# Experts' weights laid out by consecutive rows, token rows and gate products stored to match, one low part in four of the up projections on GpSimd

## The chip, the cores and the metric

The kernel runs on one core of a Trainium2 chip. The metric is device time in microseconds (us) of one launch. Before the change the median of three runs is 2925.77 us (2919.05 to 2926.43). One more execution was taken with the hardware profiler; all rows below come from it. Engines are named as in the profile: PE (TensorE), ACT (ScalarE), DVE (VectorE), POOL (GpSimd), SP (SyncE, which here only issues DMAs).

## The reference, cut to what matters

The program is two transformer blocks on 1024 tokens of 1024 features, all in float32. The change touches the last stage alone, a mixture of 32 experts of which each token uses two:

```python
xf = _rmsnorm(h, norm_g).reshape(t, d)              # t = 1024 tokens, d = 1024
...                                                 # a router picks 2 of 32 experts for each token
def expert_block(args):
    xb, e = args                                    # 128 token rows of one expert
    hid = jax.nn.silu(xb @ w_gate[e]) * (xb @ w_up[e])   # 1024 -> 512, twice
    return hid @ w_down[e]                          # 512 -> 1024
...
y = jnp.zeros((t, d), out.dtype).at[token_of].add(out)   # scaled by the gate and added to the token
```

Each sum over features may run in any order of the features, if the rows of the weights and the columns of the tokens are taken in the same one.

## The kernel before, in words

**Precision.** Every float32 product is made of three fast matmuls (`mm3`, lines 197 to 199): each operand x is split into a high part, x rounded to the fast format, and a low part, x minus the high part. In the profile the high part of a weight is `wdh` (ACT, line 1762), the low part `wdl` (DVE, line 1763). One call of `expert_parts` makes both for a piece of 128 x 1024 numbers (two rows of 128 of the sum, 512 columns each). The tiles `wdh` and `wdl` have four buffers each, so the splitting runs at most four pieces ahead of PE.

**One expert** takes twelve pieces: four for the gate projection (`pg`), four for the up projection (`pu`), two times two for the down projection (`pd`). Each piece feeds six matmuls of 512 columns. Besides, PE transposes the gathered token rows (`xg`, line 1780) and the hidden rows (`hd`, line 1802); ACT and DVE split the results (`exh`, `exl`, `hdh`, `hdl`, lines 148 and 149, read from PSUM); ACT makes the silu (line 1798), DVE the product with the up projection (line 1799), and ACT scales the output rows `y` (line 1818). Two output halves of an expert are computed while the next expert's gate projection is already being split: the down projection of expert e-1 comes after the up projection of expert e.

**Order.** The framework orders each engine's instructions at build time; at run time each engine goes strictly in that order and waits on semaphores. In the first dozen experts DVE and PE also make, in small steps, a table for experts with more than 128 tokens (`overflow`, lines 1706 to 1736).

**Weights.** `expert_weights` loads each of the three matrices of an expert as two halves of 1 MB into a ring of 13 slots of 128 x 2048 numbers (SP's queue, line 1754; six of the loads go through POOL's queue). A slot is loaded again when all pieces of it have been split. In the view `(k p) n -> p k n` partition p gets rows p, p+128, p+256, ... of the matrix, so a half is four separate runs of 512 numbers (2 KB) in each partition for gate and up, two runs of 1024 numbers (4 KB) for down.

**Tokens.** `norm` (lines 1544 to 1551) writes the normalized rows `xf` in two halves with a GpSimd product (line 1550) and stores them to `d_xf`, eight tiles of 128 tokens. POOL gathers an expert's rows from there by an indirect DMA three experts ahead (`xg`, line 1768), and adds an expert's result to the output by another (`out<-y`, line 1819).

Of the kernel before, what the change touches and what calls it, by code (L numbers as in the profile page):

```python
# [8 lines left out]
F32 = mybir.dt.float32  # L9
# [4 lines left out]
AF = mybir.ActivationFunctionType  # L14
ALU = mybir.AluOpType
# [4 lines left out]
P = 128  # L20
# [31 lines left out]
class Kernel:  # L52
# [1483 lines left out]
    def ffn_rows(self, p, pst, rk, tab):  # L1536

        nc = self.nc

        rs, lgs = {}, {}  # L1540
        group = {t: g for g in ROUTED for t in g}

        def norm(t, z):
            r = rs[t] = self.tl(p, [P, 1], tag="rn", bufs=3)
            nc.vector.tensor_copy(r, self.rms_rstd(p, z, D, EPS2, self.tl(p, [P, D], BF, tag="scr", bufs=1)))
            x = self.tl(p, [P, D], tag="xf", bufs=1)
            for s in (slice(0, 512), slice(512, D)):
                u = self.tl(p, [P, 512], tag="nrow", bufs=2)
                nc.vector.tensor_scalar(u, z[:, s], r, None, op0=ALU.mult)
                nc.gpsimd.tensor_tensor(x[:, s], u, self.gffn[:, s], op=ALU.mult)  # L1550
            nc.gpsimd.dma_start(self.d_xf[t * P:(t + 1) * P], x)

        def logits(t, z):
            xt = self.tl(p, [P, 8, P], tag="xt", bufs=1)
            for i in range(2):
                ps = self.tl(pst, [P, 4, P], tag="tp", bufs=2)
                for j in range(4):
                    nc.tensor.transpose(ps[:, j], z[:, (4 * i + j) * P:(4 * i + j + 1) * P], self.ident)
                self.evac(i, xt[:, 4 * i:4 * i + 4], ps)
            pl = self.tl(pst, [P, 512], tag="lg", bufs=1)  # L1560
            for k in range(8):
                nc.tensor.matmul(pl[:, :36], xt[:, k], self.wr[:, k], start=k == 0, stop=k == 7)
            g = group[t]
            if t == g[0]:
                lgs[g] = self.tl(p, [P, len(g), 36], tag="lgs", bufs=2)
            nc.vector.scalar_tensor_tensor(lgs[g][:, t - g[0]], pl[:, :36], rs.pop(t), self.rb, op0=ALU.mult, op1=ALU.add)

        def place(t, z):
            g = group[t]
            if t == g[-1]:  # L1570
                self.route(p, lgs.pop(g), g)
                for x in g:
                    for y in range(x):
                        nc.tensor.matmul(rk[:, x], self.onesb, self.asum[:, y], start=y == 0, stop=False)
                    nc.tensor.matmul(rk[:, x], self.trib, self.asum[:, x], start=x == 0, stop=True)

                self.slots(p, g, rk, tab)
        return [norm, logits, place]

    def route(self, p, lg, tiles):  # L1580
# [157 lines left out]
    def expert_weights(self, src, after=None):  # L1738

        r = []  # L1740
        for w in src:
            w = w.rearrange("(k p) n -> p k n", p=P)
            k = w.shape[1] // 2
            r.append([])
            for i in range(2):
                x = self.tl(self.wp[0 if self.wslot < W0 else 1 + (self.wslot == W0 or self.wslot > W0 + 8)], [P, 2048], tag=f"w{self.wslot}").rearrange("p (k n) -> p k n", k=k)
                self.wslot = (self.wslot + 1) % W1
                queue = self.nc.sync
                self.early -= 1
                if after is not None and self.early < 0:  # L1750
                    self.nc.vector.tensor_copy(x[:, 0, 0:1], after)
                    queue = self.nc.gpsimd
                with self.tc.issue_after(self.behind) if self.early >= 0 and self.behind else nullcontext():
                    d = queue.dma_start(x, w[:, i * k:(i + 1) * k])
                self.behind = d.ins
                r[-1].append(x)
        return r

    def expert_parts(self, w):
        nc = self.nc  # L1760
        wh, wl = [self.tl(self.ep, [P, 2, 512], F32R, tag=n, bufs=4) for n in ("wdh", "wdl")]
        nc.scalar.copy(wh, w)  # L1762
        nc.vector.tensor_tensor(wl, w, wh.bitcast(F32), op=ALU.subtract)  # L1763
        return wh, wl

    def expert_gather(self, idx, xg):
# [17 lines left out]
    def expert_up(self, x, w, tag):  # L1784

        ps = self.tl(self.eps, [P, 512], tag=tag)
        for g in range(4):
            wh, wl = self.expert_parts(w[g // 2][:, 2 * (g % 2):2 * (g % 2) + 2])
            for j in range(2):
                k = 2 * g + j  # L1790
                self.mm3(ps, (x[0][:, k], x[1][:, k]), (wh[:, j], wl[:, j]), k == 0, k == 7)
        return ps

    def expert_hidden(self, pg, pu):
        nc = self.nc
        hd = self.tl(self.ep, [P, 512], tag="hd", bufs=2)
        hh, hl = [self.tl(self.ep, [P, 4, P], F32R, tag=n, bufs=2) for n in ("hdh", "hdl")]
        nc.scalar.activation(hd, pg, AF.Silu)
        nc.vector.tensor_tensor(hd, hd, pu, op=ALU.mult)
        ps = self.tl(self.ept, [P, 4, P], tag="tp")  # L1800
        for f in range(4):
            nc.tensor.transpose(ps[:, f], hd[:, f * P:(f + 1) * P], self.ident)
        self.split_gain(hh, hl, ps)
        return hh, hl
# [216 lines left out]
```

## Time and profile before

| | |
|---|---|
| median of 3 runs | 2925.77 us |
| profiled execution, its own time | 2920.82 us |
| its span in the trace | 2919.0 us |
| PE busy | 2759.6 us, 95% of the span |
| DVE busy | 1866.7 us, 64% |
| ACT busy | 1335.9 us, 46% |
| POOL busy | 468.6 us, 16% |
| DMA issued by SP | 377.69 MB, 225672 packets |
| stretch of the experts | about 2290 to 2919 us |

The shares are means over stages with different limits; the experts' stage, the last fifth of the span, has its own. There the outputs `out<-y` are issued by POOL once for each of the 32 experts, so the distance between two of them is the time that an expert takes.

### The profile page before, as it was taken

To read this page: it belongs to the slowest core of one execution; us is meant where nothing else is said; L and a number is where in the kernel's file an instruction comes from. 1 tells how busy PE (TensorE), PEld (TensorE's weight loads), DVE (VectorE), ACT (ScalarE), POOL (GpSimd) and SP (SyncE) were. 2 spreads that over 40 slices of the span, in tenths; PEclk is the share of its full clock that TensorE was granted. 3 is DMA by queue.
4 is the path that set the end of the run, shared out by engine and by line. 5 is a ranking of instruction groups with operands and counts; after the bars stand their busy time and mean duration, and the time that the engine had idled before them with its cause. 6 is when DMAs were issued, how large, how long until landed. Compare 5 with 4: busy or idle time off the path is not lost. (4 is left out here: it accounts for less than half of the span.)

```text
span 2919.0 us, 36892 instructions
## 1 busy us (share of the span) xinstructions
PE 2759.6 (95%) x13590; PEld 2168.0 (74%) x13590; DVE 1866.7 (64%) x3709; ACT 1335.9 (46%) x2295; POOL 468.6 (16%) x416
## 2 busy tenths in 40 slices
PE   7999999978999999999799999899999799999997
PEld 4875667756888888887686777688768688877776
DVE  6655554697534444437963767645555799988886
ACT  5644443512211221112333766624441488877776
POOL 0043201054101111103310100000003311111111
PEclk9999999989999999999999999999999899999999
DMA  8563333411211111111124212232235799999996
GB/s 283 178 200 106 112 106 120 137 54 51 65 37 50 58 58 44 48 44 61 66 96 130 87 55 80 69 131 102 65 119 195 263 353 348 346 345 349 350 347 216
DMA packets 245950, 432.55 MB, mean 148 GB/s; under 512 B 45924, under 2 KB 95492, under 8 KB 245384
## 3 DMA queue, kind: packets, MB, share of 16 engines
q1 hardware_dynamic: 225672, 377.69, 38.1%
q0 software_dynamic: 20096, 52.49, 5.6%
q8 instruction: 108, 1.77, 0.3%
q14 instruction: 74, 0.61, 0.1%
HBM read 380.79 MB, written 66.08 MB: 153 GB/s over the span
## 5 line engine op out<-in xcount | busy, mean ns | idle before, releaser
L1763 DVE TENSOR_TENSOR wdl<-w,wdh 128x1024 fp32r<-128x1024 f32 x384 | 458.1, 1222 | 63.1 <-ACT wdh L1762 57.3
L1762 ACT CAST wdh<-w 128x1024 fp32r<-128x1024 f32 x384 | 391.6, 1051 | 96.0 <-DMA w<-in_w_e_gate 38.9
L197 PE MATMUL mm<-whi,x 128*128 128x512 f32 (+1 forms) x1008 | 407.6, 405 | 20.0 <-DVE y L869 17.8
L198 PE MATMUL mm<-wlo,x 128*128 128x512 f32 (+1 forms) x1008 | 404.0, 401 | 1.5 <-DVE wlo L165 1.5
L199 PE MATMUL mm<-whi,x 128*128 128x512 f32 (+1 forms) x1008 | 401.2, 398 | 0.0
L164 ACT CAST whi<-raw 128x1024 fp32r<-128x1024 f32 (+1 forms) x111 | 113.9, 1044 | 401.3 <-PE m L199 263.7
L197 PE MATMUL mm<-x,whi 128*128 128x512 f32 (+1 forms) x592 | 233.7, 395 | 4.2 <-ACT relu L932 4.2
L165 DVE TENSOR_TENSOR wlo<-raw,whi 128x1024 fp32r<-128x1024 f32 (+1 forms) x111 | 158.4, 1433 | 119.7 <-ACT whi L164 118.3
L197 PEld LDWEIGHTS mm<-whi,x 128*128 128x128 f32 x1008 | 193.0, 191 | 55.1 <-DVE y L869 18.2
L199 PE MATMUL mm<-x,wlo 128*128 128x512 f32 (+1 forms) x592 | 232.1, 392 | 0.0
L198 PE MATMUL mm<-x,whi 128*128 128x512 f32 (+1 forms) x592 | 231.9, 392 | 0.0
L198 PEld LDWEIGHTS mm<-wlo,x 128*128 128x128 f32 x1008 | 192.7, 191 | 37.9 <-DVE wlo L165 4.1
L199 PEld LDWEIGHTS mm<-whi,x 128*128 128x128 f32 x1008 | 192.7, 191 | 34.1 <-issue 0.8
L981 DVE TENSOR_TENSOR acc<-acc,m 128x512 f32<-128x512 f32 x128 | 87.8, 686 | 195.4 <-PE m L199 195.2
L198 PE MATMUL m<-wlo,hidh 128*128 128x512 f32 x512 | 200.8, 392 | 0.5 <-DVE wlo L165 0.5
L199 PE MATMUL m<-whi,hidl 128*128 128x512 f32 x512 | 200.7, 392 | 0.0
L197 PE MATMUL m<-whi,hidh 128*128 128x512 f32 x512 | 200.3, 391 | 0.0
L970 POOL TENSOR_TENSOR raw<-raw,gt 128x1024 f32<-128x1024 f32 x32 | 85.8, 2694 | 516.8 <-DMA raw<-in_w_ff 516.8
L197 PEld LDWEIGHTS mm<-x,whi 128*128 128x128 f32 (+1 forms) x592 | 110.4, 186 | 30.1 <-ACT relu L932 5.2
L596 ACT ACTIVATE e<-sc,nm 128x256 f32<-128x256 f32 (+6 forms) x128 | 96.4, 755 | 79.0 <-PE tp L667 43.4
L199 PEld LDWEIGHTS mm<-x,wlo 128*128 128x128 f32 (+1 forms) x592 | 110.2, 186 | 25.2 <-issue 0.8
L198 PEld LDWEIGHTS mm<-x,whi 128*128 128x128 f32 (+1 forms) x592 | 110.3, 186 | 24.8 <-issue 1.1
(572 smaller groups left out, 5851.4 us busy)
## 6 DMA issues: line engine op xcount, KB each, us to landing
w<-in_w_e_gate SPq DMA_DIRECT2D x62, 1024.0 KB
w<-in_w_e_up SPq DMA_DIRECT2D x62, 1024.0 KB
w<-in_w_e_down SPq DMA_DIRECT2D x62, 1024.0 KB
raw<-in_w_ff SPq DMA_DIRECT2D x64, 512.0 KB
araw<-in_w_ada SPq DMA_DIRECT2D x48, 512.0 KB
raw<-in_w_in SPq DMA_DIRECT2D x36, 512.0 KB
raw<-in_w_ckv SPq DMA_DIRECT2D x16, 512.0 KB
x<-in_x SPq DMA_DIRECT2D x8, 512.0 KB
```

What stands on the lines that cost most here:

```text
L164: nc.scalar.copy(hi, raw)
L165: nc.vector.tensor_tensor(lo, raw, hi.bitcast(F32), op=ALU.subtract)
L197: mm(ps, lh, rh, start=start, stop=False)
L198: mm(ps, lh, rl, start=False, stop=False)
L199: mm(ps, ll, rh, start=False, stop=stop)
L596: nc.scalar.activation(e, ps, AF.Exp, bias=nm, accum_out=l)
L970: lambda raw: nc.gpsimd.tensor_tensor(raw, raw, gt, op=ALU.mult)) for f in range(4)]
L981: nc.vector.tensor_tensor(acc[t][:, ns], acc[t][:, ns], ps, op=ALU.add)
L1762: nc.scalar.copy(wh, w)
L1763: nc.vector.tensor_tensor(wl, w, wh.bitcast(F32), op=ALU.subtract)
```

## The change

Four edits, in the functions printed above.

1. The weights' view becomes `(p k) n -> p k n`: partition p gets k consecutive rows, so each half is a single run of 8 KB in each partition.
2. So that the token columns meet the same rows, `xf` is stored permuted: column p*8+k goes to place k*128+p. The GpSimd product writes with a stride of 128 numbers.
3. So that the hidden columns meet the rows of the down projection, silu and product are written to `hd` in the order f, p from columns p*4+f of PSUM, which are read with a stride of 4.
4. The third of the four pieces (g == 2) of the gate and of the up projection has its low part made by GpSimd in place of VectorE: two of an expert's twelve.

```diff
@@ norm, in ffn_rows
                 nc.vector.tensor_scalar(u, z[:, s], r, None, op0=ALU.mult)
-                nc.gpsimd.tensor_tensor(x[:, s], u, self.gffn[:, s], op=ALU.mult)
+                v = x.rearrange("r (k p) -> r p k", k=8)[:, s.start // 8:s.stop // 8]
+                nc.gpsimd.tensor_tensor(v, u.rearrange("r (p k) -> r p k", k=8),
+                                        self.gffn[:, s].rearrange("r (p k) -> r p k", k=8), op=ALU.mult)
             nc.gpsimd.dma_start(self.d_xf[t * P:(t + 1) * P], x)
@@ expert_weights
-            w = w.rearrange("(k p) n -> p k n", p=P)
+            w = w.rearrange("(p k) n -> p k n", p=P)
@@ expert_parts
-    def expert_parts(self, w):
+    def expert_parts(self, w, eng=None):
         wh, wl = [self.tl(self.ep, [P, 2, 512], F32R, tag=n, bufs=4) for n in ("wdh", "wdl")]
         nc.scalar.copy(wh, w)
-        nc.vector.tensor_tensor(wl, w, wh.bitcast(F32), op=ALU.subtract)
+        (eng or nc.vector).tensor_tensor(wl, w, wh.bitcast(F32), op=ALU.subtract)
@@ expert_up
-            wh, wl = self.expert_parts(w[g // 2][:, 2 * (g % 2):2 * (g % 2) + 2])
+            wh, wl = self.expert_parts(w[g // 2][:, 2 * (g % 2):2 * (g % 2) + 2], self.nc.gpsimd if g == 2 else None)
@@ expert_hidden
-        nc.scalar.activation(hd, pg, AF.Silu)
-        nc.vector.tensor_tensor(hd, hd, pu, op=ALU.mult)
+        blocks = lambda x: x.rearrange("r (p f) -> r f p", f=4)
+        hd4 = hd.rearrange("r (f p) -> r f p", f=4)
+        nc.scalar.activation(hd4, blocks(pg), AF.Silu)
+        nc.vector.tensor_tensor(hd4, hd4, blocks(pu), op=ALU.mult)
```

**POOL's queue in the middle of the experts.** `xg` is a gather, `out<-y` the adding of a result, `wdl` a low part. Before:

```order
L1768 DMA xg_19621<-d_xf,idx 128x1024
L1819 DMA out<-y_21332,idx 1024x1024
L1768 DMA xg_19622<-d_xf,idx 128x1024
L1819 DMA out<-y_21519,idx 1024x1024
L1768 DMA xg_19578<-d_xf,idx 128x1024
L1819 DMA out<-y_21706,idx 1024x1024
```

The same queue after the change:

```order
L1772 DMA xg_19622<-d_xf,idx 128x1024
L1767 TENSOR_TENSOR wdl_20867<-w_4325_20835,wdh_20866 128x1024
L1825 DMA out<-y_20770,idx 1024x1024
L1767 TENSOR_TENSOR wdl_20920<-w_4327_20839,wdh_20919 128x1024
L1772 DMA xg_19578<-d_xf,idx 128x1024
L1767 TENSOR_TENSOR wdl_21054<-w_4373_21022,wdh_21053 128x1024
L1825 DMA out<-y_20958,idx 1024x1024
L1767 TENSOR_TENSOR wdl_21107<-w_4375_21026,wdh_21106 128x1024
```

A gather and an output still alternate; a low part of a gate projection now stands before each output, one of an up projection before each gather.

**DVE's queue around the gate projection of one of the first dozen experts.** `exl` is the low part of token rows, `oh`, `val` and `acc` belong to the overflow table. The weights' slots are w_4612 (first half of the gate matrix), w_4613 (second half), w_4614 and w_4615 (up). Before:

```order
L149 TENSOR_TENSOR exl_21878<-tp_21886,exh_21877 128x512
L1763 TENSOR_TENSOR wdl_21969<-w_4612_21955,wdh_21968 128x1024
L1763 TENSOR_TENSOR wdl_21979<-w_4612_21955,wdh_21978 128x1024
L1763 TENSOR_TENSOR wdl_21989<-w_4613_21957,wdh_21988 128x1024
L1725 TENSOR_SCALAR oh_21948<-iota_18358,rf 128x128
L1727 TENSOR_SCALAR val_21949<-iota_18358,blk,iota_18364 128x16
L1727 TENSOR_SCALAR val_21949<-iota_18358,blk,ga 128x16
L1763 TENSOR_TENSOR wdl_21999<-w_4613_21957,wdh_21998 128x1024
L1730 TENSOR_TENSOR acc<-acc,tp_21941 128x32
L1763 TENSOR_TENSOR wdl_22022<-w_4614_21959,wdh_22021 128x1024
L1763 TENSOR_TENSOR wdl_22032<-w_4614_21959,wdh_22031 128x1024
L1763 TENSOR_TENSOR wdl_22042<-w_4615_21961,wdh_22041 128x1024
```

The same place on DVE after the change:

```order
L149 TENSOR_TENSOR exl_21878<-tp_21886,exh_21877 128x512
L1767 TENSOR_TENSOR wdl_21969<-w_4612_21955,wdh_21968 128x1024
L1767 TENSOR_TENSOR wdl_21979<-w_4612_21955,wdh_21978 128x1024
L1728 TENSOR_SCALAR oh_21948<-iota_18358,rf 128x128
L1730 TENSOR_SCALAR val_21949<-iota_18358,blk,iota_18364 128x16
L1730 TENSOR_SCALAR val_21949<-iota_18358,blk,ga 128x16
L1733 TENSOR_TENSOR acc<-acc,tp_21941 128x32
L1728 TENSOR_SCALAR oh_22129<-iota_18358,rf 128x128
L1730 TENSOR_SCALAR val_22130<-iota_18358,blk,iota_18364 128x16
L1730 TENSOR_SCALAR val_22130<-iota_18358,blk,ga 128x16
L1767 TENSOR_TENSOR wdl_21999<-w_4613_21957,wdh_21998 128x1024
L1767 TENSOR_TENSOR wdl_22022<-w_4614_21959,wdh_22021 128x1024
```

The third low part of the gate (from w_4613) is gone from DVE, and the table's small steps, which were spread among the low parts, now stand together in its place. ACT's and PE's queues keep their order, and SP issues the same loads in the same order.

## Rows read from the trace of the kernel before

**Rows 1.** The page: span, DMA share and GB/s in 40 slices.

```profile
span 2919.0 us, 36892 instructions
...
DMA  8563333411211111111124212232235799999996
GB/s 283 178 200 106 112 106 120 137 54 51 65 37 50 58 58 44 48 44 61 66 96 130 87 55 80 69 131 102 65 119 195 263 353 348 346 345 349 350 347 216
```

**Rows 2.** Windows of the experts' stage: busy us of each engine, clock, DMA.

```profile
core 0: us, PE busy (x) PEld busy (x) DVE busy (x) ACT busy (x) POOL busy (x), PEclk, DMA share, GB/s
...
2360.00:2560.00 200.00, 198.15 (x944) 162.33 (x943) 191.12 (x239) 167.03 (x196) 32.39 (x22) 1.00 0.99 349
2560.00:2880.00 320.00, 310.84 (x1411) 243.25 (x1409) 274.36 (x269) 249.16 (x300) 50.18 (x30) 1.00 0.99 348
```

**Rows 3.** Timeline of POOL: outputs of experts 0, 1, 12, 29, 30 (start, us).

```profile
2335.25 1.88 POOL L1819 DMA_INDIRECT out<-y,idx  x1 [4.40 <-ACT y L1818]
...
2352.98 1.82 POOL L1819 DMA_INDIRECT out<-y,idx  x1 [5.17 <-ACT y L1818]
...
2556.22 1.80 POOL L1819 DMA_INDIRECT out<-y,idx  x1 [5.17 <-ACT y L1818]
...
2882.43 2.03 POOL L1819 DMA_INDIRECT out<-y,idx  x1 [17.09 <-ACT y L1818]
...
2899.83 1.79 POOL L1819 DMA_INDIRECT out<-y,idx  x1 [15.38 <-ACT y L1818]
```

**Rows 4.** Waits from 2560 to 2880 us: total us, times, longest.

```profile
DVE wdl L1763 <- ACT wdh L1762: 42.9, 63, 2.3
ACT wdh L1762 <- DMA w<-in_w_e_gate: 33.8, 21, 2.6
...
ACT wdh L1762 <- DMA w<-in_w_e_up: 11.7, 17, 1.8
```

**Rows 5.** Waits from 2360 to 2560 us.

```profile
DVE wdl L1763 <- ACT wdh L1762: 6.3, 17, 1.5
ACT wdh L1762 <- DMA w<-in_w_e_gate: 5.0, 6, 2.0
```

**Rows 6.** Windows near the program's start, where DMA is full too.

```profile
18.00:20.00 2.00, 2.00 (x12) 1.67 (x11) 2.00 (x5) 1.01 (x3) 0.00 (x0) 1.00 1.02 420
...
28.00:30.00 2.00, 2.00 (x15) 0.60 (x14) 2.00 (x7) 1.26 (x4) 0.00 (x0) 1.00 1.05 383
```

**Rows 7.** SP's issues there: x has rows of 4 KB, raw and araw 2 KB.

```profile
12.08 3.80 SPq L414 DMA_DIRECT2D x<-in_x  x7
16.14 4.12 SPq L375 DMA_DIRECT2D araw<-in_w_ada  x4
21.18 3.18 SPq L160 DMA_DIRECT2D raw<-in_w_ckv  x3
```

**Rows 8.** DVE by line from 2560 to 2880 us: busy us, mean ns.

```profile
L1763 DVE TENSOR_TENSOR wdl<-w,wdh 128x1024 fp32r<-128x1024 f32 x199 | 235.3, 1221 | 44.9 <-ACT wdh L1762 42.9 <-PE pd L199 1.1
L149 DVE TENSOR_TENSOR exl<-tp,exh 128x512 fp32r<-128x512 f32 x34 | 21.8, 683 | 0.0
...
L1799 DVE TENSOR_TENSOR hd<-hd,pu 128x512 f32<-128x512 f32 x17 | 11.6, 680 | 0.0
```

**Rows 9.** Timeline of the feed-forward stage, POOL and DVE (start, us).

```profile
733.68 1.23 DVE L165 TENSOR_TENSOR wlo<-raw,whi 128x1024 fp32r<-128x1024 f32 x1 [0.26 <-ACT whi L164]
...
1136.84 2.39 POOL L970 TENSOR_TENSOR raw<-raw,gt 128x1024 f32<-128x1024 f32 x1 [74.09 <-DMA raw<-in_w_ff]
...
1147.01 2.76 POOL L970 TENSOR_TENSOR raw<-raw,gt 128x1024 f32<-128x1024 f32 x1 [1.43 <-DMA raw<-in_w_ff]
...
1147.77 3.08 DVE L165 TENSOR_TENSOR wlo<-raw,whi 128x1024 fp32r<-128x1024 f32 x1 [0.26 <-ACT whi L164]
```

**Rows 10.** Timeline of POOL: the last tile of xf, the first gather.

```profile
2280.39 2.77 POOL L1550 TENSOR_TENSOR xf<-nrow,gffn 128x512 f32<-128x512 f32 x2 [6.26 <-DVE nrow L1549]
2283.46 0.58 POOL L1551 DMA_DIRECT2D d_xf<-xf  x1 [0.30 <-POOL xf L1550]
...
2294.16 1.91 POOL L1768 DMA_INDIRECT xg<-d_xf,idx  x1 [9.16 <-DVE f L1710]
```

**Rows 11.** DMA issues by line: KB each, us to landing.

```profile
d_xf<-xf POOLq DMA_DIRECT2D x8, 512.0 KB, 4.2
```

**Rows 12.** ACT's silu by line, 2350 to 2880 us.

```profile
L1798 ACT ACTIVATE hd<-pg 128x512 f32<-128x512 f32 x28 | 16.8, 600 | 7.3 <-PE pg L199 7.3
```

## The prediction

> **What bounds the kernel now.** The page comes first. Its line of GB/s [rows 1] shows DMA far from full until the last fifth of the span and then flat near 348 GB/s, with nine tenths or more busy: the experts. All four edits touch that stage or what feeds it, so the rest of the program is left as it is.
>
> Next the pace of an expert, from the outputs that POOL issues once for each [rows 3]. From expert 0 to 12 it is (2556.22 - 2335.25) / 12 = 18.41 us, from 12 to 29 (2882.43 - 2556.22) / 17 = 19.19 us, then 17.40 us for the last distance. Over all 30 distances the mean is 18.82 us. The shortest shown is 17.73 us, from expert 0 to 1. I take it as what PE needs when nothing is late, since PE's busy time fills nearly all of the first window (198.15 of 200 us).
>
> Then the windows say which engine goes with which pace [rows 2]. Up to expert 12 PE has 99% and DVE 191.12 of 200 us: 96%, or 17.59 us per expert. So the first dozen are bound by PE and DVE together. Behind it DVE falls to 274.36 of 320 us, 16.45 us per expert, and PE shows gaps. The waits name the reason: ACT's split of a weight waits for the load of the gate matrix 33.8 us and of the up matrix 11.7 us [rows 4], against 5.0 us in the first window [rows 5]. There ACT is late because the weight is late, and DVE is late because ACT is (42.9 us against 6.3). The ring of 13 slots has run empty and the late experts go at DMA's pace: 348 GB/s times 19.19 us is 6.68 MB per expert. That fits: the weights are six transfers of 1 MB, and the rest is token rows.
>
> **Edit 1, the weights' layout.** It adds and removes no instruction; it turns four runs of 2 KB (two of 4 KB) per partition into one of 8 KB. No row shows 8 KB runs, so I bound the rate from rows where DMA is full too. In the middle of the 3.67 MB of x, rows of 4 KB, it moves 420 GB/s; a few us later, with the 2 KB runs of araw and raw, 383 GB/s [rows 6, 7]. The experts' own mix gives 348. If length does nothing, the rate stays 348 (19.19 us per expert). With 383 the 6.68 MB take 17.4 us, with 420 15.9 us. A loss cannot be excluded by rows, since consecutive runs also change which addresses are read together, but nothing points to one. I take 400 to 420: the runs become longer than those of x. At any rate over 6.68 / 17.73 = 377 GB/s the loads cease to set the pace, so what is taken above that does not matter.
>
> The page DMA: Bandwidth & Descriptors of the Trainium skill (section Where 436 GB/s comes from) speaks against this edit: between HBM and SBUF, it says, the HBM side at about 358 GB/s binds. By that rule the 348 is nearly the limit whatever the runs, and this edit gives nothing. The trace disagrees, with 420 GB/s for x [rows 6]; but those are other loads, so this case stays as a rival below.
>
> **Edit 4, low parts on GpSimd.** DVE loses two of twelve low parts: 2 x 1.22 = 2.44 us per expert [rows 8]. Alone this would make DVE quick: 17.59 becomes 15.15, 16.45 becomes 14.01. But the feed-forward stage shows what a GpSimd operation on two tiles of the same size does to a DVE operation on two. The low part there takes 1.23 us alone; begun 0.76 us after GpSimd's it takes 3.08 us, and it ends 1.08 us after GpSimd's end (1147.01 + 2.76 = 1149.77; 1147.77 + 3.08 = 1150.85) [rows 9]. It stood still until GpSimd was done. So each moved part takes 1.22 us from DVE and gives back up to GpSimd's whole duration, which is 2.39 us alone and 2.76 us in the disturbed case [rows 9].
>
> Without any cover DVE's sum is 16.45 - 2.44 + 2 x 2.39 = 18.79 us for late experts and 19.93 us for early ones (19.53 and 20.67 with 2.76). What can cover it: GpSimd's part runs beside DVE operations that are not held. All held ones in rows 9 have two inputs in SBUF. Four DVE operations of an expert read PSUM (two `exl`, `hdl`, the product `hd`), 0.68 us each [rows 8]. No row shows one of these beside GpSimd, held or not, so the cover is between 0 and 4 x 0.68 = 2.72 us. In the order, the low part of the gate's third piece follows close behind the two `exl` and DVE runs late there, so I expect half of those two to lie beside it: 0.68 us. In the early experts the table's small steps now stand together in that very place on DVE; they are the 17.59 - 16.45 = 1.14 us by which early DVE is fuller, and I let half of them be covered too. Late: 18.79 - 0.68 = 18.11, with handing over 18.2 us. Early: 19.93 - 0.68 - 0.57 = 18.68, taken as 18.6 us.
>
> [...]
>
> POOL's own queue bears the new work: some 2 x 2.4 us more in an expert of 18, where it is busy 32.39 of 200 us now [rows 2]. The gate's part is queued ahead of the output of the expert before, which has three buffers for `y`; the up projection's part stands behind that output, whose issue takes 1.8 to 2 us [rows 3]. That output waits for `y`, ready about when PE begins the next gate projection, so the part has the rest of a gate projection to be in time. A gather held back is three experts early.
>
> **Edits 2 and 3, the permuted stores.** Instruction counts stay; only strides change, and no row shows these strides. For `xf` the bounds are the 2.77 us that a tile's two products take now and twice that; the last tile is in memory at 2283.46 + 4.2 = 2287.7 us and the first gather starts at 2294.16 [rows 10, 11]. 6.5 us of cover hide 2.8 us. For silu (0.60 us [rows 12]) and product (0.68 us) the bounds are the same time and twice it; a gain is excluded, since no element is saved. Doubling would put 0.68 us on DVE per expert, 20 us over 30. I take no change, and 2 us for the whole of edits 2 and 3.
>
> **The sum.** Early: 12 x (18.6 - 18.41) = +2.3. Late: 17 x (18.2 - 19.19) = -16.8. Last distance: 18.2 - 17.4 = +0.8. With 2 us for the strides: -11.7 us, or 2909.1 against the profiled execution's 2920.82. That execution lies 4.95 us under the median, so against the median it is 2914 us. My first two terms are rounded against the change, so I state 2913.
>
> **The rivals.**
> 1. *The shared access decides* (slower). DVE and GpSimd never overlap. Early 12 x (19.93 - 18.41) = +18.2, late 17 x (18.79 - 19.19) = -6.8, last +1.4: +13 us, 2939; with 2.76 us per part +35 us, 2961. For it: rows 9, and DVE at 96% in the first window. Against: late DVE has 14% of idle time. It turns slower as soon as the mean over the 30 distances passes 18.82 us.
> 2. *The loads are not relieved.* 348 GB/s is a limit of something other than run length. Late experts stay at 19.19 us, and slower early ones merely leave the ring fuller: 0 to +5 us, 2928. For it: the flat 345 to 350 GB/s [rows 1]. Against: 420 in rows 6.
> 3. *Everything is covered.* The four PSUM operations lie beside GpSimd in full and PE alone binds. Late 17 x (17.73 - 19.19) = -24.8, early 12 x (18.0 - 18.41) = -4.9: -30 us, 2896. For it: late DVE would need only 18.79 - 2.72 = 16.1 us. Against: this needs each part to start just when such an operation comes.
>
> **How the numbers follow.** Chances: forecast 0.47 (its own range 2900 to 2925), rival 1 0.22, rival 2 0.16, rival 3 0.15. A measurement of this kernel tells about 0.3% from no change, 8.8 us: faster is under 2917, slower over 2934.5. Faster: 0.33 of the forecast's 0.47 and rival 3, 0.48. Slower: 0.17 of rival 1, 0.03 of rival 2, 0.02 of the forecast's upper tail, 0.22. The same: 0.30. The range of 2893 to 2943 takes in rival 3, rival 2 and rival 1 with the 2.39 us; the 2961 is left out.
>
> **What would show it.** Right: in the experts' windows GB/s over 377 or DMA's busy share under 0.95, no ACT wait for gate or up loads behind 2560 us, some DVE low parts of 2 to 3.5 us where GpSimd's run, late experts at about 18.2 us, early ones at 18.4 to 18.9. Wrong: GB/s flat at 348 with the waits for loads as before (rival 2); early experts over 19.5 us with DVE full (rival 1); DVE low parts all at 1.22 us, or GpSimd's part well over 2.8 us, which no term here holds.

## The result and the profile after

The median after is 2946.09 us (2945.58 to 2951.69, 4 runs) against 2922.41 (2917.96 to 2926.43, 4 runs): a ratio of 1.0087, 95% interval 1.0071 to 1.0103. That is slower by 0.9%, and outside the forecast range of 2893 to 2943. The profiled execution has a span of 2944.2 us, 25.2 more than before.

POOL's timeline, columns as in [rows 3], gives the outputs of experts 0, 4, 13, 20, 30 and 31 after the change.

```profile
2337.71 2.43 POOL L1825 DMA_INDIRECT out<-y,idx  x1 [0.17 <-ACT wdh L1766]
...
2414.32 2.41 POOL L1825 DMA_INDIRECT out<-y,idx  x1
...
2595.41 2.42 POOL L1825 DMA_INDIRECT out<-y,idx  x1 [0.15 <-ACT wdh L1766]
...
2722.74 2.39 POOL L1825 DMA_INDIRECT out<-y,idx  x1 [0.17 <-issue]
...
2924.01 1.77 POOL L1825 DMA_INDIRECT out<-y,idx  x1 [9.29 <-ACT y L1824]
2932.22 1.56 POOL L1825 DMA_INDIRECT out<-y,idx  x1 [6.44 <-issue]
```

Before, the outputs of experts 0 and 30 start at 2335.25 and 2899.83 [rows 3]; those of 4, 13, 20 and 31 are these:

```profile
2407.32 2.47 POOL L1819 DMA_INDIRECT out<-y,idx  x1 [5.17 <-ACT y L1818]
...
2575.16 1.88 POOL L1819 DMA_INDIRECT out<-y,idx  x1 [5.54 <-ACT y L1818]
...
2713.85 1.86 POOL L1819 DMA_INDIRECT out<-y,idx  x1 [8.17 <-ACT y L1818]
...
2906.98 1.55 POOL L1819 DMA_INDIRECT out<-y,idx  x1 [5.35 <-ACTq L1861]
```

The differences place the 25.2 us:

| stretch | before, us | after, us | difference |
|---|---|---|---|
| to the output of expert 0 | 2335.25 | 2337.71 | +2.5 |
| experts 0 to 4 | 72.07 | 76.61 | +4.5 |
| experts 4 to 13 | 167.84 | 181.09 | +13.3 |
| experts 13 to 20 | 138.69 | 127.33 | -11.4 |
| experts 20 to 30 | 185.98 | 201.27 | +15.3 |
| behind the output of expert 30 | 19.17 | 20.19 | +1.0 |

So the change gains among the later experts, where it was expected to gain, but for seven of them only (and the experiments show that it is hardly the new layout that makes these seven quick). The distances between outputs show three regimes: 20.34 to 20.40 us for each expert from 5 to 13, 18.18 to 18.20 from 13 to 20, and, after one of 15.98, 20.15 to 21.17 in the last nine up to expert 30. A window from each regime, columns as in [rows 2]:

```profile
2440.00:2560.00 120.00, 108.77 (x518) 88.75 (x518) 109.22 (x126) 91.08 (x105) 43.90 (x25) 1.00 0.85 313
2600.00:2720.00 120.00, 119.18 (x558) 97.09 (x557) 110.66 (x95) 101.85 (x120) 63.40 (x27) 1.00 0.97 366
2760.00:2880.00 120.00, 107.79 (x486) 84.06 (x485) 99.61 (x81) 86.96 (x104) 41.33 (x21) 1.00 0.85 327
```

In the middle PE is nearly full. In the other two it idles 11.23 and 12.21 of 120 us, and DMA is at 0.85, so the loads are not what is late; of ACT's waits for them [rows 4, 5] one is left between 2360 and 2880 us:

```profile
ACT wdh L1766 <- DMA w<-in_w_e_gate: 0.4, 1, 0.4
```

On the queue of the weights the packets fall from 225672 to 170120.

**Experts 5 to 13.** Waits from 2440 to 2560 us (total us, times, longest):

```profile
PEld tp L1731 <- DVE val L1730: 13.9, 6, 2.3
PE tp L1731 <- DVE val L1730: 11.2, 6, 1.9
```

PE's whole idle time of 11.23 us is one wait: six times, once in each expert, a matmul of the overflow table stands at the head of PE's queue and waits for DVE's `val`. The timeline of one such place shows why (start, us, engine; all rows but these four left out):

```profile
2450.19 2.50 POOL L1767 TENSOR_TENSOR wdl<-w,wdh 128x1024 fp32r<-128x1024 f32 x1 [4.01 <-ACT wdh L1766]
...
2450.38 2.39 DVE L1728 TENSOR_SCALAR oh<-iota,rf 128x128 f32<-128x128 f32 x1
...
2452.70 0.28 DVE L1730 TENSOR_SCALAR val<-iota,blk,iota 128x16 f32<-128x16 f32 x1
...
2453.23 0.41 PE L1731 MATMUL tp<-val,oh 128*128 128x32 f32 x2 [1.87 <-DVE val L1730]
```

`oh` is issued 0.19 us after GpSimd's low part and ends with it (2452.77 against 2452.69). It took 2.39 us here and 1336 ns on average over the window, since every second one is held; before it took 281 ns (first line: after, 2440 to 2560 us; second: before, 2360 to 2560):

```profile
L1728 DVE TENSOR_SCALAR oh<-iota,rf 128x128 f32<-128x128 f32 x12 | 16.0, 1336 | 0.0
...
L1725 DVE TENSOR_SCALAR oh<-iota,rf 128x128 f32<-128x128 f32 x15 | 4.2, 281 | 0.0
```

It is a small step of 128x128 numbers with one tile and one column of scalars as inputs. The table's matmul waits 1.87 us, and with it everything behind it in PE's queue: the rest of the gate projection.

Of the 4.5 us lost in experts 0 to 4, 3.2 lie in the one distance from expert 3 to 4 (21.32 us, before 18.11). There two steps that prepare the table are held in the same way, `hd` (before 0.69 us) and `blk` (before 0.17):

```profile
2390.75 2.65 DVE L1709 TENSOR_TENSOR hd<-ab,base 128x512 f32<-128x512 f32 x1
...
2396.30 2.38 DVE L1714 SCALAR_TENSOR_TENSOR blk<-f,blk 128x16 f32<-128x16 f32 x1
```

Behind them PE waits 2.5 us for DVE's low parts (2394 to 2416 us).

**Experts 20 to 30.** Waits from 2760 to 2880 us:

```profile
ACT hd L1804 <- PE pg L199: 17.3, 6, 3.1
...
PEld pu L198 <- POOL wdl L1767: 8.3, 6, 1.5
PEld pg L198 <- POOL wdl L1767: 8.0, 6, 1.9
...
PE pg L198 <- POOL wdl L1767: 6.5, 6, 1.5
PE pu L198 <- POOL wdl L1767: 5.7, 6, 1.0
```

6.5 and 5.7 are 12.2 us: again all that PE idles. Here it is GpSimd's low parts themselves that come late. The timeline of one gate projection:

```profile
2800.32 0.48 PE L197 MATMUL pg<-wdh,exh 128*128 128x512 f32 x1
2800.39 0.69 ACT L1824 ACTIVATE y<-pd,gate 128x512 f32<-128x512 f32 x1 [0.41 <-PE pd L199]
...
2801.05 0.58 ACT L148 CAST hdh<-tp 128x512 fp32r<-128x512 f32 x1
...
2801.54 3.89 ACT L1766 CAST wdh<-w 128x1024 fp32r<-128x1024 f32 x4
...
2802.68 2.70 POOL L1767 TENSOR_TENSOR wdl<-w,wdh 128x1024 fp32r<-128x1024 f32 x1
...
2805.43 0.50 PE L198 MATMUL pg<-wdl,exh 128*128 128x512 f32 x1 [1.00 <-POOL wdl L1767]
```

PE begins the projection at 2800.32, but ACT makes the high part of the third piece only behind `y` and `hdh`, at 2801.54; GpSimd's part runs from 2802.68 to 2805.38, and PE wants it at 2804.43. A part of DVE's 1.22 us [rows 8], begun at the same time, would end at 2803.9 (an estimate). Before the change ACT goes in this order here too (at one place `y` at 2767.97 us, `hdh` at 2768.55, the casts from 2769.01); what it costs without GpSimd's part is the subject of an experiment below.

**What stayed as expected.** By line, from 2560 to 2880 us, columns as in [rows 8]; silu is of 2350 to 2880 us, as in [rows 12], and GpSimd's part is the page's own row:

```profile
L1767 DVE TENSOR_TENSOR wdl<-w,wdh 128x1024 fp32r<-128x1024 f32 x165 | 238.3, 1486 | 39.7 <-ACT wdh L1766 39.7
L149 DVE TENSOR_TENSOR exl<-tp,exh 128x512 fp32r<-128x512 f32 x34 | 21.8, 680 | 0.0
...
L1805 DVE TENSOR_TENSOR hd<-hd,pu 128x512 f32<-128x512 f32 x16 | 10.8, 676 | 0.0
```

```profile
L1804 ACT ACTIVATE hd<-pg 128x512 f32<-128x512 f32 x27 | 16.2, 599 | 19.3 <-PE pg L199 19.3
```

```profile
L1767 POOL TENSOR_TENSOR wdl<-w,wdh 128x1024 fp32r<-128x1024 f32 x64 | 172.9, 2702 | 136.4 <-ACT wdh L1766 130.9
```

Silu and product cost the same with strides (599 and 676 ns against 600 and 680). DVE's low parts grew from 1221 to 1486 ns by the hold; GpSimd's takes 2.70 us. Over the whole stage DVE's low parts take 445.6 us where they took 458.1: of the 64 x 1.22 = 78 us that were moved, the holds on the other parts give 66 back.

### The profile page after: what moved, and what is told of

It reads as the page before. It is cut to its first block, busy times and chain, and to the rows that moved or that the text cites. A ratio compares the mean times of both kernels' runs of the same rounds, so it can differ in the third digit from the quotient of the medians.

```text
span 2944.2 us, 36983 instructions
## 1 busy us (share of the span) xinstructions
PE 2758.2 (94%) x13590; PEld 2172.3 (74%) x13590; DVE 1879.0 (64%) x3645; ACT 1340.3 (46%) x2295; POOL 641.1 (22%) x480
## 5 line engine op out<-in xcount | busy, mean ns | idle before, releaser
L1767 DVE TENSOR_TENSOR wdl<-w,wdh 128x1024 fp32r<-128x1024 f32 x320 | 445.6, 1432 | 67.1 <-ACT wdh L1766 67.1
L197 PE MATMUL mm<-whi,x 128*128 128x512 f32 (+1 forms) x1008 | 408.2, 405 | 19.3 <-DVE y L869 17.2
L1767 POOL TENSOR_TENSOR wdl<-w,wdh 128x1024 fp32r<-128x1024 f32 x64 | 172.9, 2702 | 136.4 <-ACT wdh L1766 130.9
L197 PEld LDWEIGHTS mm<-x,whi 128*128 128x128 f32 (+1 forms) x592 | 110.3, 186 | 28.4 <-ACT relu L932 4.0
## 6 DMA issues: line engine op xcount, KB each, us to landing
w<-in_w_e_gate SPq DMA_DIRECT2D x62, 1024.0 KB, 10.2
```

What stands on the lines that cost most here:

```text
L197: mm(ps, lh, rh, start=start, stop=False)
L1767: (eng or nc.vector).tensor_tensor(wl, w, wh.bitcast(F32), op=ALU.subtract)
```

## The experiments

The time at which POOL issues the first gather varies from 2291.2 to 2300.5 us between these executions, though they differ hardly at all up to there. So beside the medians I compare a stage, from the start of the first gather to the end of the span: 624.8 us before (2919.0 - 2294.16), 650.3 after (2944.2 - 2293.88). A stage is of the one profiled execution of each kernel. All ratios are to the kernel before on the same chip (its medians there are 2920.97 to 2923.33).

| kernel | median, us | ratio, 95% interval | stage, us |
|---|---|---|---|
| before | 2922.41 | | 624.8 |
| after | 2946.09 | 1.0071 to 1.0103 | 650.3 |
| edits 1 to 3 | 2906.59 | 0.9929 to 0.9962 | 607.6 |
| edit 4 alone | 2952.17 | 1.0092 to 1.0125 | 652.1 |
| after, table later | 2944.55 | 1.0069 to 1.0102 | 648.9 |
| after, POOL's order | 2948.62 | 1.0069 to 1.0107 | 649.7 |
| after, ACT's order | 2933.95 | 1.0022 to 1.0048 | 633.7 |
| after, `oh` on ACT | 2938.45 | 1.0040 to 1.0074 | 640.1 |
| after, both of these | 2922.99 | 0.9994 to 1.0014 | 624.1 |
| edits 1 to 3, ACT's order | 2902.33 | 0.9910 to 0.9943 | 605.1 |
| edits 1 to 3, both of these | 2902.65 | 0.9914 to 0.9947 | 606.2 |

The theory after the result: the layout by itself gains as forecast, and edit 4 loses more than that, by two separate waits on PE. The rivals: the layout itself costs something (its strides, its addresses); GpSimd's parts are late because of POOL's own queue; the table is late because of its place, not because of the hold.

**The two halves apart.** Edits 1 to 3 with all low parts on DVE:

```diff
-            wh, wl = self.expert_parts(w[g // 2][:, 2 * (g % 2):2 * (g % 2) + 2], self.nc.gpsimd if g == 2 else None)
+            wh, wl = self.expert_parts(w[g // 2][:, 2 * (g % 2):2 * (g % 2) + 2])
```

> Edits 1 to 3 alone, all low parts on VectorE. Theory A (the layout relieves the loads, the GpSimd parts cost all that was lost): no ACT wait for weights, experts 0 to 12 at about 18.4 us as before, later ones at 17.8 to 18.3 in place of 19.2, 15 to 24 us under the kernel before (2898 to 2908). Rival B (the strided silu, product and store cost): early experts over 18.8 us and silu or product longer than 0.60 and 0.68 us, time at 2922 or above. Rival C (run length does not matter to DMA): GB/s flat at 348, late experts at 19.2, same time as before.

And edit 4 put into the kernel before, with its old layout:

> Edit 4 alone on the old layout. Theory A: early experts with table steps at 20.4 us as in the changed kernel, the last ten at 20.4 too, the middle between 18.2 (while the ring, filled by the slow start, lasts) and 19.2: 20 to 35 us over before, 2942 to 2957. Rival B (the layout is what cost): within 0.3% of before.

The layout alone gives 0.9946, edit 4 alone 1.0108. The stage is 17.2 us shorter with the one and 27.3 longer with the other. In edit 4 alone the pace is 20.35 to 20.39 us for eight early experts and 18.17 to 18.20 for six in the middle, as after: these regimes belong to edit 4, whatever the layout. That holds for the quick middle too. With the old layout and 352 GB/s it has PE as full as after:

```profile
2600.00:2720.00 120.00, 119.05 (x556) 96.63 (x555) 109.14 (x94) 99.84 (x118) 63.95 (x26) 1.00 1.00 352
```

From expert 13 to 20 edit 4 alone takes 128.84 us, after 127.33, before 138.69. So 9.9 of the 11.4 us gained there need no new layout. While the early experts are slow the loads run ahead: from 2440 to 2560 us SP's queue waits 91.7 us for DVE's low parts to free a slot, before 19.3. Beside edit 4 the layout is worth 1.8 us of stage (652.1 to 650.3), without it 17.2.

The layout alone has 17.73 us where the table is done, with PE full and DMA at 373 GB/s:

```profile
2560.00:2660.00 100.00, 100.00 (x478) 83.14 (x478) 93.84 (x94) 86.24 (x103) 15.64 (x13) 1.00 0.98 373
```

Its waits from 2660 to 2880 us, where the last experts take 17.5 to 19.3 us, show that loads are late again, against the expectation, though less than before (13.2 of 220 us against 45.5 of 320 [rows 4]):

```profile
ACT wdh L1766 <- DMA w<-in_w_e_gate: 9.1, 6, 2.5
ACT wdh L1766 <- DMA w<-in_w_e_up: 4.1, 5, 1.2
```

DMA's share is 0.91 in this window, and SP's queue waits 126.7 us of it for DVE's low parts, that is, for a slot to come free. So the rate alone does not make them late.

**What run length does to the loads.** Two kernels whose experts compute so little that the loads alone set the pace, one in each layout:

```diff
-        nc.scalar.copy(wh, w)
-        (eng or nc.vector).tensor_tensor(wl, w, wh.bitcast(F32), op=ALU.subtract)
-        return wh, wl
+        self.flip = not getattr(self, 'flip', False)
+        nc.scalar.copy(wh, w) if self.flip else nc.vector.tensor_copy(wh, w)
+        return wh, wh
...
-                self.mm3(ps, (x[0][:, k], x[1][:, k]), (wh[:, j], wl[:, j]), k == 0, k == 7)
+                self.nc.tensor.matmul(ps, x[0][:, k], wh[:, j], start=k == 0, stop=k == 7)
```

> The old layout with the computing of the experts cut: only the high times high matmul of each piece, no low parts of weights, high parts by ACT and VectorE in turn, so that the loads bound the stage. Theory A (runs of 2 and 4 KB): GB/s in the stage near 350. Rival B (the 348 was the demand of a slower consumer, not DMA's limit): 380 or more.

> The same cut in the new layout. Theory A (8 KB runs are quicker): 380 to 420 GB/s, the stage 5 to 15% shorter than in the old layout. Rival B (run length does nothing): GB/s as in the old layout.

One run each. The windows of the old layout, then of the new one:

```profile
2360.00:2560.00 200.00, 113.85 (x402) 77.88 (x402) 80.06 (x168) 96.64 (x122) 28.39 (x22) 0.75 0.98 350
2560.00:2800.00 240.00, 139.34 (x440) 95.85 (x441) 80.97 (x125) 118.95 (x149) 33.66 (x24) 0.69 0.98 347
2320.00:2360.00 40.00, 21.37 (x96) 14.82 (x95) 16.60 (x28) 22.04 (x31) 11.13 (x9) 0.79 1.01 359
```

```profile
2360.00:2560.00 200.00, 125.26 (x414) 86.11 (x414) 82.70 (x172) 101.82 (x129) 28.36 (x23) 0.72 0.94 363
2560.00:2800.00 240.00, 140.01 (x453) 95.19 (x454) 82.85 (x127) 121.36 (x152) 35.10 (x25) 0.72 0.94 365
2320.00:2360.00 40.00, 26.96 (x112) 18.89 (x110) 19.02 (x32) 24.83 (x34) 12.66 (x11) 0.80 1.02 404
```

From 2320 to 2360 us, with DMA full in both, the new layout moves 404 GB/s and the old one 359. Behind that it moves 364 against 350 and 347, 4 to 5% more, but with DMA not quite full. Per full share, an estimate, that is 350 / 0.98 = 357 GB/s against 364 / 0.94 = 387: 8% more. The stage is 3.4% shorter (595.0 us against 615.8), under the expected 5 to 15%. So the layout does limit the loads; whether it does so by the length of the runs or by which addresses are read together, these two kernels do not separate. The 387 is under the 400 to 420 that the forecast took, and over the 377 that it needed.

**The table of the first dozen experts.** The changed kernel, with the table's steps moved behind expert 17:

```diff
-                if e > 1:
+                if e > 17:
                     next(more, None)
```

> The changed kernel with the table steps made during experts 18 to 30 in place of 2 to 14. Theory A (a table step held behind GpSimd's low part, with PE waiting for it, makes the early experts slow): experts 1 to 13 fall from 20.4 to about 18.2 us, experts 18 to 20 rise to 20.4, the last ten stay at 20.4 or rise by up to 2 us. Total between 15 us less and 10 us more than the changed kernel. Rival B (in the early experts the sum of VectorE and GpSimd is the bound, table or not): experts 1 to 13 at 19.9 us or more.

The first 17 distances fall to 18.18 to 18.20 us, and those that now hold the table rise to between 20.8 and 23.2. The 21.32 us of expert 4 is 18.19 now as well. So the early loss belongs to the table and goes where it goes; the sum (2944.55) is nearly unchanged. Whether the hold on `oh` does it, or the place of the table's matmuls, this leaves open. The next edit makes `oh` on ACT, as 1 minus a squared difference cut off at 0, and leaves it where it is (`neg` is made once from `rf`):

```diff
+        neg, one = t("neg", 2, NT), t("one", 1)
...
-                X.tensor_scalar(oh, self.iota, self.rf[:, c, x:x + 1], None, op0=ALU.is_equal)
+                nc.scalar.activation(oh, self.iota, AF.Square, bias=neg[:, c, x:x + 1])
+                nc.scalar.activation(oh, oh, AF.Relu, scale=-1.0, bias=one)
```

> The changed kernel, with one step of the overflow table moved: the 128x128 one-hot `oh` is made by ACT (a Square with bias and a Relu) and no longer by DVE, where it takes 0.28 us in the kernel before and 1.4 us on average in the changed one. Everything else stays, so the table's matmuls keep their place in PE's queue. If experts 5 to 13 take 20.37 us because GpSimd's low part holds `oh` on DVE, they fall to between 18.2 and 18.8 us, nine distances save 14 to 19 us, and the time is 2927 to 2932. If they take it because PE meets the table's matmuls at a bad place of its queue, whoever makes `oh`, they stay at 20 us or more and the time stays at 2943 to 2949. The last ten experts stay at 20.3 to 20.5 us by either.

Experts 5 to 13 take 18.85 to 18.97 us. That is 1.4 us less than 20.37, and a little over the expected 18.2 to 18.8, as the time (2938.45) is over the expected 2927 to 2932. The matmuls kept their place, so the place does not make these 1.4 us. The hold itself is not gone, though; it falls on the next small step. Here it is `val`, of 128x16 numbers:

```profile
2447.51 2.62 POOL L1771 TENSOR_TENSOR wdl<-w,wdh 128x1024 fp32r<-128x1024 f32 x1 [3.94 <-ACT wdh L1770]
2447.78 2.38 DVE L1734 TENSOR_SCALAR val<-iota,blk,iota 128x16 f32<-128x16 f32 x1
...
2450.50 0.38 PE L1735 MATMUL tp<-val,oh 128*128 128x32 f32 x2 [0.43 <-DVE val L1734]
```

PE now waits 0.43 us and not 1.87. In the window DVE has no idle time left:

```profile
2440.00:2560.00 120.00, 117.40 (x562) 96.03 (x561) 120.00 (x122) 104.93 (x139) 50.55 (x25) 1.00 0.91 337
```

But a full DVE is not what holds the pace at 18.9 us: the kernel with both causes removed, below, has the same pace in this window with DVE at 112.80.

**The last ten experts.** My first suspicion was POOL's queue: there the output stands ahead of GpSimd's gate part and waits up to 9.6 us for `y`. In this edit each GpSimd part is issued ahead of the output and of the gather:

```diff
+                if add:
+                    with tc.issue_after(self.low):
+                        add()
...
+                    with tc.issue_after(self.low):
+                        gather(e + 3)
```

> The changed kernel with POOL's queue held to one order throughout: low part of gate, output of the expert before, low part of up, gather. Theory A (the last ten experts are slow since there output and gather, which wait for PE, stand ahead of the low parts): the last ten fall from 20.4 to 18.2 to 18.6 us, 18 to 22 us under the changed kernel, the early ones stay at 20.4. Rival B (the last ten are slow for another reason, PE's own order or the loads): they stay at 20.4 and the time is that of the changed kernel.

That theory fell: the last ten stay at 20.14 to 21.30 us (but for the first and last of them), and the time is 2948.62. With neither ahead of it on POOL, the part waits for ACT's high part:

```profile
2808.54 2.38 POOL L1767 TENSOR_TENSOR wdl<-w,wdh 128x1024 fp32r<-128x1024 f32 x1 [8.89 <-ACT wdh L1766]
```

So the next edit holds ACT's queue in the order that it has in the middle experts: the second half of `y` behind the cast of the third gate piece, `hdh` behind that of the fourth, silu behind the fourth cast of the up projection. Its core (`casts` lists the casts so far, `end` makes the second half of `y`, `add` is the output):

```diff
+                    with tc.issue_after(self.casts[-2]):
+                        add = end()
+                    add()
...
-                    h = self.expert_hidden(*last[0])
+                    h = self.expert_hidden(*last[0], (tc.issue_after(up), tc.issue_after(self.casts[-1])))
```

> The changed kernel with ACT's queue held in the last ten experts to the order of the middle ones: the second output half of the expert before, and the split of its hidden rows, behind the high parts of the gate's third and fourth piece, the silu behind the last high part of the up projection. Theory A (in the last ten ACT makes the high part of the third piece only when PE has begun that projection, so GpSimd's 2.4 us in place of VectorE's 1.2 are exposed): the last ten fall from 20.45 to 18.2 to 18.8 us, total 15 to 22 us under the changed kernel, PE's waits for GpSimd's low part fall under 3 us in the last 120 us. Rival B (loads, PE's own order): the last ten stay above 19.8.

The five distances from expert 25 on are 18.22, 18.23, 18.18, 18.18 and 16.04 us, and PE is full there (69.95 of 70 us from 2830 on). The stage is 16.6 us shorter than after. The edit also puts the output behind GpSimd's gate part on POOL; the run before shows that this alone gains nothing. The early experts stay at 20.37, so the two waits are separate. Four distances behind expert 21 stay at 19.4 to 20.3 us, against the expectation. Of the waits from 2760 to 2880 us those for the gate's part are gone and some for the up projection's are left:

```profile
PEld pu L198 <- POOL wdl L1767: 5.8, 6, 1.7
...
PE pu L198 <- POOL wdl L1767: 3.5, 3, 1.2
```

What orders these four otherwise was not tried.

**The control, and the best version.** The same order on ACT with all low parts on DVE:

> The layout alone (all low parts on VectorE) with the same hold on ACT's queue. Theory A: VectorE's short low part hides ACT's late order already, so the last ten gain little: 18.26 us falls to 17.8 to 18.2, 0 to 5 us under the layout alone. Rival B (the loads still set the pace there): no change, and ACT waits for weights are seen.

Without GpSimd's parts the order is worth 2.5 us of stage (607.6 to 605.1), with them 16.6: ACT's old order costs mainly beside GpSimd's part. The control is not a clean one, since in its last experts ACT waits for loads too (19.6 us from 2660 to 2880), which can hide a part of what the order is worth there. At 0.9927 (0.9910 to 0.9943) this kernel beats both.

**Both causes removed.** The changed kernel with `oh` on ACT and ACT's order held, and the same two edits without GpSimd's parts:

> The changed kernel with `oh` on ACT and ACT's queue held in the order of the middle experts to the end, so that both suspected causes are gone. If these two are the whole of what the forecast missed, the experts take 18.2 us nearly everywhere (the four at about 19.5 us behind expert 20 may stay) and the time is 2908 to 2918, about the 2913 that was forecast. If a third cause is there, one stretch of experts stays at 20 us and the time is 2925 or more. By either it stays above the layout alone with the same order on ACT (2902), since 18.2 us is 0.45 more than the 17.73 of the layout alone.

> Edits 1 to 3 with all low parts on DVE, ACT's order held as above, and `oh` on ACT as well. The control for the two runs beside it: nothing on GpSimd can hold DVE here. If `oh` costs only what it takes on DVE (0.28 us, once in each early expert), the first 13 distances shrink by at most 0.3 us each and the time is 2898 to 2903. If moving it to ACT is itself a cost or a gain of more than that (ACT's queue, or the table's place on PE), the early distances of 18.2 to 18.6 us move by over 0.5 us, and what the other two runs gain has to be corrected by it.

The changed kernel with both comes to 2922.99 us, the time of before (0.9994 to 1.0014), and its stage is 26.2 us shorter than after; the single edits gave 10.2 and 16.6, so the two causes add up. It was expected at 2908 to 2918: these two are most of what the forecast missed, not all. No stretch is back at 20.37 us: experts 5 to 13 take 18.93 to 19.02, the middle 18.18 to 18.20, the last 18.20 to 18.21 (the four of 19.4 to 20.3 are there again, and so is the 21.31 of expert 4). In the control `oh` on ACT gains nothing (606.2 against 605.1), so its gain beside GpSimd's parts comes from the hold. GpSimd's two parts per expert still cost 624.1 - 606.2 = 17.9 us with both causes gone: by the outputs 3.0 us up to the first, 5.0 in experts 0 to 5, 5.2 from 5 to 13, 0.1 from 13 to 20, 4.8 from 20 to 30. From 13 to 20 the control runs at 17.73 us until its loads are late again, and the two come out even. Of the 5.0 us, 3.2 are the distance to expert 4 (21.31 against 18.15), with `hd` and `blk` held as shown above. From 5 to 13 the distances are 0.65 us over the control's (18.95 against 18.30), and PE still waits for the table, about 0.6 us in an expert; DVE has idle time there (waits, then the window):

```profile
PE tp L1735 <- DVE val L1734: 3.7, 7, 0.9
```

```profile
2440.00:2560.00 120.00, 117.22 (x559) 95.79 (x559) 112.80 (x121) 104.82 (x140) 58.30 (x26) 1.00 0.92 342
```

## Why the prediction was wrong

- **Edit 1 relieves the loads: right by itself.** The layout alone is 0.54% faster, and the waits for loads are gone from the changed kernel. The rate was mis-sized (an estimated 387, not 400 to 420): runs of 8 KB came under the 420 of x's 4 KB. In the changed kernel this has no consequence, since its DMA share is 0.85 to 0.97, but the layout then gains little either (1.8 us of stage beside edit 4), and most of the late gain, from expert 13 to 20, comes without it.
- On the rate: rival 2's rule (the Trainium skill, DMA: Bandwidth & Descriptors, section Where 436 GB/s comes from) is that between HBM and SBUF the HBM side binds at about 358 GB/s. The new layout's 404 GB/s for 40 us and 363 to 365 behind that say otherwise.
- **Edits 2 and 3 cost at most 2 us: right.** No strided operation became longer by more than 1%, and the first gather starts no later (2293.88 against 2294.16 us [rows 10]), though this start varies by 9 us between executions. The 2 us were too many.
- **"Early: 19.93 - 0.68 - 0.57 = 18.68": the first step that failed.** I read the table's small steps as cover, work that could run beside GpSimd's part. They are among the steps that are held: `oh` grew from 281 to 1336 ns. The other cover hardly occurred: of the 128 DVE steps that read PSUM (`exl`, `hdl`, `hd`) only five began beside a GpSimd part. They took 680 to 693 ns, so they were not held. And I added up DVE, while the loss is on PE, whose queue has the table's matmuls ahead of a projection. Measured: 20.37 us from expert 5 on. By the first twelve distances the term was +16.3 us (237.30 against 220.97), not +2.3. The evidence was in the order printed ahead of the prediction: the steps stood together exactly where GpSimd's part falls. With `oh` off DVE the pace is 18.9; that it lies near the 18.68 is luck, since PE's waits make it and not DVE's sum.
- On that step: the page SBUF — State Buffer of the Trainium skill (section Who interferes with whom) counts VectorE's tensor_scalar among the instructions that can contend with GpSimd, when it runs in one of its 2-port modes. The 2.39 us of `oh` agree with that; which mode it ran in, no run here shows. The forecast had asked only whether a step has two inputs in SBUF.
- **"The part has the rest of a gate projection to be in time": the second step that failed.** It was true of the order in the middle experts, and I let that hold to the end. In the last ten ACT casts the third piece after PE has begun the projection; DVE's 1.22 us hid that and GpSimd's 2.70 do not. So "Late: 18.79 - 0.68 = 18.11, with handing over 18.2 us" held for seven experts of seventeen, and the late term was +2.6 us (328.85 against 326.21), not -16.8. The last distance was +2.75, not +0.8. With +2.5 up to the first output and +1.0 behind that of expert 30 the three terms give the 25.2 us.
- **The 18.2 us of the middle: the number was right, the reason was not.** I took it from a full DVE, at 18.11 us per expert. There DVE has 110.66 of 120 us, 16.8 per expert, so the number came out by luck. PE is nearly full, and its weight loads wait 3.4 us in the window for GpSimd's gate part, 0.57 us in each of six experts. That is about the 0.46 between 18.19 and the 17.73 of the layout alone; no run isolates it.
- **The sum's rounding.** It says that both first terms are rounded against the change. The early one, 18.68 taken as 18.6, is rounded for it, by 12 x 0.08 = 1 us; this decides nothing.
- **The rivals.** Rival 1 (2939 to 2961) holds the time, and it had the sign. Its mechanism is half of it: DVE is held, as it said, but in the changed kernel DVE is not full in any of the three regimes (109.22, 110.66 and 99.61 of 120 us); PE waits for single results. Rival 2 fell with the two load kernels and the layout alone; rival 3 with the held steps, since some cover failed everywhere.
- What stays open: why four experts behind expert 21 stay at 19.4 to 20.3 us with ACT's order held, and what makes up the rest of the last 17.9 us. The holds around the table, seen in the trace, account for some 8 of them; no run removes these.

## What to carry to other kernels

Moving an operation to a slower engine that has time to spare has to be judged by latency, not by busy time: for each place where it stands, ask when its input comes and when its consumer, on an engine that goes strictly in order, wants it; and ask it for every order in which the program's queues go, since one loop had three regimes here. GpSimd's part held small steps of VectorE as long as large ones here, so a 0.3 us step in front of a matmul cost PE 1.9 us. And run the halves of a combined change apart: here the one gave 0.5% by itself, and beside the other, which cost 1.1%, nearly nothing.

## What the hardware showed that I had not expected

- VectorE steps of 0.28 us with one tile and one or two columns of scalars were held for GpSimd's whole operation: `oh` 2.39 us, `val`, of 16 columns, 2.38. Steps that read PSUM were not: `exl` and `hdl` beside GpSimd took 680 to 693 ns.
- GpSimd's low part takes 2.38 to 2.40 us at best and 2.98 on average in the densest stretch (2600 to 2720 us); what slows it was not tested.
- The layout with runs of 8 KB in place of 2 and 4 KB gave 404 GB/s in place of 359 for 40 us, and an estimated 387 in place of 357 per full share over 440 us of loads.
- Reads from PSUM with a stride of 4 cost ACT and DVE nothing (599 and 676 ns against 600 and 680), and writes to SBUF with a stride of 128 cost GpSimd next to nothing (a median of 1412 ns against 1402).
